# A decoder block on one core: attention rows turned four steps behind their scores, values ahead of the next pair's transposes

## The chip, the cores and the metric

The kernel runs on one core of a Trainium2 chip. A core has five engines, each with an instruction stream of its own: TensorE (PE in the profile, with PEld for its weight loads), VectorE (DVE), ScalarE (ACT), GpSimd (POOL), and SyncE (SP), which here issues the DMAs. They meet through semaphores. Matrix products go to PSUM, which this kernel cuts into eight banks of 128 x 512 float32; DVE and ACT read them from there. The metric is the device time of one launch in microseconds.

## The reference, cut to what matters

One decoder block on 512 tokens of width 1024: a norm, one projection, a retention branch and an attention branch, a gated merge, and a feed-forward part. The change lies in the attention branch alone, eight heads of 64:

```python
def forgetting_attention(q, k, v, log_f):
    scale = 1.0 / math.sqrt(d)
    c = jnp.cumsum(log_f, axis=1).transpose(0, 2, 1)
    ...
        s = jnp.einsum('bhqd,bhkd->bhqk', q_blk, kh).astype(jnp.float32) * scale
        s = s + c_blk[..., None] - c[:, :, None, :]
        mask = pos_k[None, :] <= pos_q[:, None]
        s = jnp.where(mask[None, None], s, -jnp.inf)
        p = jax.nn.softmax(s, axis=-1)
        return jnp.einsum('bhqk,bhkd->bhqd', p.astype(vh.dtype), vh)
```

## The kernel before

Float32 products are made of three products of a high and a low part each (`three`), so nearly every matmul runs as high x high, high x low and low x high.

The program is one stream on TensorE. From `pinned[0] = True` to `pinned[0] = False` the matmuls keep the order in which the code is written; where the code is not pinned, and on all other engines, a scheduler sets the order when the kernel is built, and each engine then works through its list in that order. The projection comes first, then retention, then attention (about 169 to 248 us of the profiled execution), then the merge and the feed-forward part.

Attention runs in steps `s`, one for each row block of one head: `chain` holds the 32 triples (a, e, i), pair `a` 0 to 3, head `e` 0 or 1 in the pair, block `i` of 128 queries from 3 down to 0. Here "row s" is the work on `chain[s]`, (i+1) x 128 columns wide. A row goes through these hands:

- `fox_scores` (L481): two matmuls into a bank tagged `sc` (there are two of these). DVE adds the bias row `cb` and takes the minimum (L499, a custom operation into `pr`, with `nm` read after it); ahead of it POOL adds the mask to one 128 x 128 square of `cb` (L491). ACT takes the exponential of `pr` in place (L501, with the row sums read after it), DVE takes the reciprocal `ri` (L502) and scales `pr` (L503).
- `fox_turn` (L506): TensorE transposes the i+1 squares of `pr` into a bank tagged `tp` (two of these as well, shared with `fox_prep`), and the bank is copied to `pT`: by DVE where i is 3 (L516), by ACT otherwise (L518).
- `fox_values` (L520): once both heads of a pair are turned, eight products of `pT` with `vf`, the two heads by turns, into an `sc` bank; ACT and DVE take it out (L171, L172, `ofh` and `ofl`). The first product of each head reads the part of `pT` that the last turned row, i = 0, writes.
- `fox_prep` (L458): for the next pair, at steps with `s % 8` of 3 and 5, TensorE transposes `kf` (part 0) or `qf` (part 1) into a `tp` bank. ACT copies halves of it out (`tk`, L467 and L468, four copies; `tq`, L477, two), and DVE makes the remainders (`kl`, L469; `tq`, L478, two each).

Between these, `fill(us)` puts other products into the stream: the projection's gate columns (`acc<-xh,wh` in the rows; `acc` names four further banks), whose inputs do not hang on attention. They last until step 20. The products of the next stage (`acc<-orh,...`, `acc<-ofh,...`) are not pinned, and the scheduler puts some of them into the stream from step 15 on. With the gate columns come weights, cast by ACT (`wh`, L152) and subtracted by DVE (`wl`, L153).

The loop at L629 says what a step does: scores of row s, at two steps in eight `fill` and `fox_prep`, the turn of row s - LAG with LAG = 3, the values of a pair at step 8a + 11, and a `fill`. `PT`, `PR` and `CBUF` are the numbers of buffers of `pT`, `pr` and `cb`.

Of the kernel before, what the change touches and what calls it, by code (L numbers as in the profile page):

```python
# [53 lines left out]
def block_kernel(ctx: ExitStack, tc, x, xT, c_early, c_tab, c_late, w_qf, w_tok, w_a, w_y, w_o, w_gu, w_dn, w_dh, out):  # L54
# [16 lines left out]
    def mm(o, **kw):  # L71
        in_order(nc.tensor.matmul(o, **kw))  # L72

    def turn(o, src):
        in_order(nc.tensor.transpose(out=o, in_=src, identity=ident))  # L75

    def f32(ap):
        return ap.bitcast(F32)
# [12 lines left out]
    def bank(tag):  # L91
        return ps.tile([P, 512], F32, name=tag, tag=tag, bufs={"acc": 4, "sc": 2, "tp": 2}[tag])
# [35 lines left out]


    WU, WP = 1056, 1152  # L130
    RAW, WB, SG, PT, PR, TB, CBUF = 2, 3, 8, 3, 4, 2, 3
    PREP = [3, 5]
    RF, CF, PF, SF, LAG = (5.32, 4.64, 5.6, 4.6, 11.2), (3.0, 2.0, 2.26, 4.0), 5.9, (0.83, 1.03, 1.77, 1.6), 3

    raw_pools, part_pools, turns = [wp] * RAW, [wp] * WB, [0, 0]

# [33 lines left out]
    def split_ps(src, h, l):  # L170
        nc.scalar.copy(out=h, in_=src)  # L171
        tt(out=l, in0=src, in1=f32(h), op=ALU.subtract)  # L172
# [282 lines left out]
    ra, rb = slice(0, FD), slice(FD, P)  # L455
    fox = {}

    def fox_prep(a, part):  # L458

        if part == 0:  # L460
            tk = [fwk.tile([P, S], F32R, name="tk", tag=f"tk{e}", bufs=TB) for e in range(2)]
            kl = kls[a % TB]
            pk = bank("tp")
            for t in range(NT):
                turn(pk[:, t * P:(t + 1) * P], kf[:, t, a * P:(a + 1) * P])
            for e, (r, o) in enumerate(((ra, rb), (rb, ra))):
                act(out=tk[e][r], in_=pk[r], func=AF.Copy, scale=gk[r])  # L467
                act(out=tk[e][o], in_=pk[r], func=AF.Copy, scale=gk[r])  # L468
                stt(out=kl[e][r], in0=pk[r], scalar=gk[r], in1=f32(tk[e])[r], op0=ALU.mult, op1=ALU.subtract)  # L469
            fox["k", a] = tk, kl  # L470
        else:
            tq = [fwk.tile([P, S], F32R, name="tq", tag=f"tq{e}", bufs=TB) for e in range(2)]
            pq = bank("tp")
            for t in range(NT):
                turn(pq[:, t * P:(t + 1) * P], qf[:, t, a * P:(a + 1) * P])
            for e, (r, o) in enumerate(((ra, rb), (rb, ra))):
                act(out=tq[e][r], in_=pq[r], func=AF.Copy, scale=gq[r])  # L477
                stt(out=tq[e][o], in0=pq[r], scalar=gq[r], in1=f32(tq[e])[r], op0=ALU.mult, op1=ALU.subtract)  # L478
            fox["q", a] = tq

    def fox_scores(a, e, i):  # L481

        tq, (tk, kl) = fox["q", a], fox["k", a]
        if i == NT - 1:
            fox["cb"] = fox_bias(2 * a + e)
            fox["pT", a, e] = fwk.tile([P, 3 * 384 + S], F32, name="pT", tag="pT", bufs=PT)
        cb = fox["cb"]
        n = (i + 1) * P
        m = max(n, 256)
        qs = slice(i * P, n)  # L490
        gp.tensor_tensor(out=cb[:, qs], in0=cb[:, qs], in1=mask, op=ALU.add)  # L491
        sc = bank("sc")
        mm(sc[:, :m], lhsT=tq[e][:, qs], rhs=tk[e][:, :m], start=True, stop=False)
        mm(sc[:, :m], lhsT=tq[e][:, qs], rhs=kl[e][:, :m], start=False, stop=True)
        pr = fwk.tile([P, S], F32, name="pr", tag="pr", bufs=PR)
        nm = sm.tile([P, 1], F32, name="nm", tag="nm", bufs=4)
        rs = sm.tile([P, 1], F32, name="rs", tag="rs", bufs=4)
        ri = sm.tile([P, 1], F32, name="ri", tag="ri", bufs=4)
        nc.vector.tensor_tensor_reduce(out=pr[:, :n], in0=cb[:, :n], in1=sc[:, :n], scale=-1.0, scalar=3e38,  # L499
                                       op0=ALU.add, op1=ALU.min, accum_out=nm)  # L500
        fox["last"] = act(out=pr[:, :n], in_=pr[:, :n], func=AF.Exp, scale=-1.0, bias=nm, accum_out=rs)  # L501
        nc.vector.reciprocal(out=ri, in_=rs)  # L502
        ts(out=pr[:, :n], in0=pr[:, :n], scalar1=ri, scalar2=None, op0=ALU.mult)  # L503
        fox["pr", a, e, i] = pr

    def fox_turn(a, e, i):  # L506

        pr, pT = fox["pr", a, e, i], fox["pT", a, e]
        pt = bank("tp")
        for j in range(i + 1):  # L510
            turn(pt[:, j * P:(j + 1) * P], pr[:, j * P:(j + 1) * P])
        row = pT[:, i * P:(i + 1) * P]
        dst = bass.AP(tensor=row.tensor, offset=row.offset, ap=[row.ap[0], [384, i + 1], [1, P]])
        src = pt[:, :(i + 1) * P].rearrange("p (j q) -> p j q", j=i + 1)
        if i == 3:
            nc.vector.tensor_copy(out=dst, in_=src)  # L516
        else:
            nc.scalar.copy(out=dst, in_=src)  # L518

    def fox_values(a):  # L520
        av = bank("sc")
        for j in range(NT):
            for e in range(2):
                mm(av[e * FD:(e + 1) * FD, j * P:], lhsT=vf[:, j, (2 * a + e) * FD:(2 * a + e + 1) * FD],
                   rhs=fox["pT", a, e][:, j * 512:j * 384 + 512], start=j == 0, stop=j == NT - 1)
        split_ps(av, ofh[:, a, :], ofl[:, a, :])
# [94 lines left out]
    for pair in kls:  # L621
        for e, o in enumerate((rb, ra)):
            gp.memset(f32(pair[e])[o], 0.0)
    fox_prep(0, 1)
    fill(CF[3])
    fox_prep(0, 0)
    fill(PF)
    chain = [(a, e, i) for a in range(4) for e in range(2) for i in reversed(range(NT))]
    for s in range(len(chain) + LAG + 2):  # L629
        if s < len(chain):  # L630
            fox_scores(*chain[s])
            if s % 8 in PREP and s // 8 < 3:
                fill(SF[0] / 2)
                fox_prep(s // 8 + 1, PREP.index(s % 8))
        if LAG <= s < len(chain) + LAG:
            fox_turn(*chain[s - LAG])
        v = s - LAG - 1
        if v >= 0 and v % 8 == 7:
            if v == 7:
                fill.until(2)  # L640
            fox_values(v // 8)
        fill(SF[chain[min(s, len(chain) - 1)][2]])
    fill.until(1)
    pinned[0] = False
# [284 lines left out]
    for g in range(4):  # L929
        if g < 3:  # L930
            ws.append(factors(w_dh[g + 1]))
        o = pf[:, HALF + 2 * g:HALF + 2 * g + 2, :].rearrange("p a (s t) -> p (a s) t", s=2)
# [135 lines left out]
```

## Time and profile before

| | |
|---|---|
| median of three timed runs | 716.09 us (715.72 to 716.59) |
| the profiled execution | 717.38 us, its span 715.6 us |
| TensorE busy | 708.9 us, 99% of the span |
| DVE, ACT, POOL busy | 509.2, 344.0, 70.1 us |
| granted TensorE clock | 1.000 over the span |

The span runs from the first to the last instruction; the rest of the time, 1.8 us, lies around it. The profiled execution was 1.3 us longer than the median. TensorE's busy time counts matmuls to their modelled ends, which overlap the next, so a short wait can hide in it; the distance from one matmul's start to the next one's shows it.

### The profile page before, as it was taken

What the parts mean: (1) busy time and instruction counts of PE and PEld (TensorE: products, weight loads), DVE (VectorE), ACT (ScalarE), POOL (GpSimd) and SP (SyncE); (2) the same over time, 40 slices, a digit from 0 to 9 for tenths busy, and PEclk for the clock granted to TensorE, in tenths of its full rate; (3) what the DMA queues carried; (4) which work ended last, traced back from release to release, by engine and by line L of the source; (5) the groups of instructions that cost most, each with busy time, mean ns of one, the idle gap of its engine ahead of it and who ended that gap; (6) DMA issues with size and microseconds to landing.
All of it is one profiled execution on the core that took longest, in us unless ns stands there. A gap on an engine that the chain in (4) does not pass through costs nothing.

```text
span 715.6 us, 10855 instructions
## 1 busy us (share of the span) xinstructions
PE 708.9 (99%) x4307; PEld 623.7 (87%) x4307; DVE 509.2 (71%) x844; ACT 344.0 (48%) x532; POOL 70.1 (10%) x90
## 2 busy tenths in 40 slices
PE   8999999999999999999999999999999999999998
PEld 6888998888777688888888999999999998888998
DVE  6333667756878673545968798899888998854684
ACT  4542434446766732233654755655665555533251
POOL 0163502121311100000220000000000000000000
PEclk9999999999999999999999999999999999999999
DMA  8632222233212023326603233322332213353112
GB/s 286 248 118 90 63 87 62 87 121 119 96 65 73 31 89 101 105 89 220 221 1 117 69 110 119 118 71 106 120 118 92 86 56 122 120 173 99 56 69 75
DMA packets 19908, 76.34 MB, mean 107 GB/s; under 512 B 2312, under 2 KB 2952, under 8 KB 16656
## 3 DMA queue, kind: packets, MB, share of 16 engines
q1 hardware_dynamic: 19712, 75.62, 31.2%
q8 instruction: 34, 0.56, 0.3%
q14 instruction: 18, 0.15, 0.1%
q10 hardware_dynamic: 144, 0.02, 0.0%
HBM read 73.52 MB, written 2.11 MB: 106 GB/s over the span
## 4 chain that ended last, share of the span: by engine, by line
PE 92%; DVE 3%; ACT 2%; issue 1%; POOL 1%; DMA 1%; SPq 0%; DVEq 0%; ACTq 0%
PE acc L72 59%; PE sc L72 27%; PE tp L72 5%; PE tp L75 2%; DVE pr L499 1%; POOL cb L491 1%; DVE pr L503 1%; DMA raw<-in_w_tok_dram 1%; ACT pr L501 1%; ACT tk L468 0%; DVE tq L478 0%; ACT tk L467 0%; DVE kl L469 0%; DVE sg L548 0%; DVE ofl L172 0%
## 5 line engine op out<-in xcount | busy, mean ns | idle before, releaser
L152 ACT CAST wh<-raw 128x1024 fp32r<-128x1024 f32 (+1 forms) x52 | 54.5, 1050 | 123.4 <-PE acc L72 97.4
L153 DVE TENSOR_TENSOR wl<-raw,wh 128x1024 fp32r<-128x1024 f32 (+1 forms) x52 | 66.6, 1282 | 48.4 <-ACT wh L152 48.3
L72 PE MATMUL sc<-xfh,cl 128*128 128x256 f32 x288 | 83.2, 289 | 0.0
L72 PE MATMUL sc<-xfh,ch 128*128 128x256 f32 x288 | 81.6, 283 | 0.0
L72 PE MATMUL sc<-xfl,ch 128*128 128x256 f32 x288 | 81.4, 283 | 0.0
L72 PE MATMUL acc<-wh,xh 128*128 128x512 f32 (+2 forms) x192 | 69.7, 363 | 0.0
L741 DVE TENSOR_TENSOR cl<-t,ch 128x1024 fp32r<-128x1024 f32 x48 | 58.6, 1222 | 13.7 <-ACT ch L741 13.6
L72 PE MATMUL acc<-wh,xl 128*128 128x512 f32 (+2 forms) x192 | 68.2, 355 | 0.0
L72 PE MATMUL acc<-wl,xh 128*128 128x512 f32 (+2 forms) x192 | 68.0, 354 | 0.0
L72 PE MATMUL acc<-xfh,ah 128*128 128x256 f32 (+1 forms) x216 | 63.9, 296 | 0.0
L72 PE MATMUL acc<-xfh,al 128*128 128x256 f32 (+1 forms) x216 | 63.7, 295 | 0.0
L72 PE MATMUL acc<-xfl,ah 128*128 128x256 f32 (+1 forms) x216 | 63.7, 295 | 0.0
L741 ACT CAST ch<-t 128x1024 fp32r<-128x1024 f32 x48 | 50.5, 1052 | 12.8 <-PE tp L72 8.0
L72 PEld LDWEIGHTS sc<-xfh,cl 128*128 128x128 f32 x288 | 55.0, 191 | 0.8 <-DVE cl L741 0.2
L72 PEld LDWEIGHTS sc<-xfh,ch 128*128 128x128 f32 x288 | 55.1, 191 | 0.1
L72 PEld LDWEIGHTS sc<-xfl,ch 128*128 128x128 f32 x288 | 55.1, 191 | 0.0
L72 PE MATMUL acc<-xh,wh 128*128 128x512 f32 x128 | 51.8, 404 | 0.0
L72 PE MATMUL acc<-xh,wl 128*128 128x512 f32 x128 | 50.0, 391 | 0.0
L72 PE MATMUL acc<-xl,wh 128*128 128x512 f32 x128 | 49.9, 390 | 0.0
L741 DVE TENSOR_TENSOR al<-raw,ah 128x1536 fp32r<-128x1536 f32 x24 | 42.2, 1757 | 6.9 <-ACT ah L741 6.9
L72 PEld LDWEIGHTS acc<-xfh,al 128*128 128x128 f32 x216 | 41.3, 191 | 1.0
L72 PEld LDWEIGHTS acc<-xfl,ah 128*128 128x128 f32 x216 | 41.3, 191 | 0.9
(294 smaller groups left out, 1796.3 us busy)
## 6 DMA issues: line engine op xcount, KB each, us to landing
raw<-in_w_gu_dram SPq DMA_DIRECT2D x21, 1024.0 KB, 4.8
raw<-in_w_tok_dram SPq DMA_DIRECT2D x16, 512.0 KB, 3.7
raw<-in_w_a_dram SPq DMA_DIRECT2D x16, 512.0 KB, 3.6
t<-in_w_dn_dram SPq DMA_DIRECT2D x14, 512.0 KB, 3.7
raw<-in_w_y_dram SPq DMA_DIRECT2D x8, 512.0 KB, 3.6
raw<-in_w_o_dram SPq DMA_DIRECT2D x8, 512.0 KB, 3.7
raw<-in_w_dh_dram SPq DMA_DIRECT2D x4, 1024.0 KB, 4.8
xf<-in_xT_dram SPq DMA_DIRECT2D x8, 256.0 KB, 5.0
```

The source lines that it names most:

```text
L72: in_order(nc.tensor.matmul(o, **kw))
L75: in_order(nc.tensor.transpose(out=o, in_=src, identity=ident))
L152: nc.scalar.copy(out=h[:, :width], in_=raw[:, :width])
L153: tt(out=l[:, :width], in0=raw[:, :width], in1=f32(h)[:, :width], op=ALU.subtract)
L491: gp.tensor_tensor(out=cb[:, qs], in0=cb[:, qs], in1=mask, op=ALU.add)
L499: nc.vector.tensor_tensor_reduce(out=pr[:, :n], in0=cb[:, :n], in1=sc[:, :n], scale=-1.0, scalar=3e38, op0=ALU.add, op1=ALU.min, accum_out=nm)
L501: fox["last"] = act(out=pr[:, :n], in_=pr[:, :n], func=AF.Exp, scale=-1.0, bias=nm, accum_out=rs)
L503: ts(out=pr[:, :n], in0=pr[:, :n], scalar1=ri, scalar2=None, op0=ALU.mult)
L741: split_to.last = nc.scalar.copy(out=h, in_=src), tt(out=l, in0=src, in1=f32(h), op=ALU.subtract)
```

## The change

Five edits. LAG goes from 3 to 4. In the loop, `fox_values` stands ahead of `fox_turn`; with the larger LAG the values of pair a come at step 8a + 12, behind the scores of that step and ahead of the turn of row 8a + 8. `pT` gets two buffers for three, `pr` six for four. In `fox_prep` the copies of a bank are all written ahead of the remainders.

```diff
-    RAW, WB, SG, PT, PR, TB, CBUF = 2, 3, 8, 3, 4, 2, 3
+    RAW, WB, SG, PT, PR, TB, CBUF = 2, 3, 8, 2, 6, 2, 3
     PREP = [3, 5]
-    RF, CF, PF, SF, LAG = (5.32, 4.64, 5.6, 4.6, 11.2), (3.0, 2.0, 2.26, 4.0), 5.9, (0.83, 1.03, 1.77, 1.6), 3
+    RF, CF, PF, SF, LAG = (5.32, 4.64, 5.6, 4.6, 11.2), (3.0, 2.0, 2.26, 4.0), 5.9, (0.83, 1.03, 1.77, 1.6), 4
@@ fox_prep
             for e, (r, o) in enumerate(((ra, rb), (rb, ra))):
                 act(out=tk[e][r], in_=pk[r], func=AF.Copy, scale=gk[r])
                 act(out=tk[e][o], in_=pk[r], func=AF.Copy, scale=gk[r])
+            for e, r in enumerate((ra, rb)):
                 stt(out=kl[e][r], in0=pk[r], scalar=gk[r], in1=f32(tk[e])[r], op0=ALU.mult, op1=ALU.subtract)
@@ 
             for e, (r, o) in enumerate(((ra, rb), (rb, ra))):
                 act(out=tq[e][r], in_=pq[r], func=AF.Copy, scale=gq[r])
+            for e, (r, o) in enumerate(((ra, rb), (rb, ra))):
                 stt(out=tq[e][o], in0=pq[r], scalar=gq[r], in1=f32(tq[e])[r], op0=ALU.mult, op1=ALU.subtract)
@@ the loop over s
-        if LAG <= s < len(chain) + LAG:
-            fox_turn(*chain[s - LAG])
         v = s - LAG - 1
         if v >= 0 and v % 8 == 7:
             if v == 7:
                 fill.until(2)
             fox_values(v // 8)
+        if LAG <= s < len(chain) + LAG:
+            fox_turn(*chain[s - LAG])
```

The number of instructions of each kind stays as it was; their order moves. TensorE's order from the scores of row 11 on, before (`acc` rows are gate columns, `sc<-tk` and `sc<-kl` scores, `tp<-ctab,kf` the transposes of k, `tp<-ctab,pr` turned rows, `sc<-pT` values):

```order
L72 MATMUL sc<-kl,tq 128x256
L75 MATMUL tp<-ctab,kf 128x128 x4
L75 MATMUL tp<-ctab,pr 128x128 x4
L72 MATMUL sc<-pT,vf 64x512 x2
L72 MATMUL sc<-pT,vf 64x384 x2
L72 MATMUL sc<-pT,vf 64x256 x2
L72 MATMUL sc<-pT,vf 64x128 x2
L72 MATMUL acc<-xh,wh 128x512
```

The same place in the changed kernel, up to the scores and the values:

```order
L75 MATMUL tp<-ctab,kf 128x128 x4
L75 MATMUL tp<-ctab,pr 128x128
L72 MATMUL acc<-xh,wh 128x512
L72 MATMUL acc<-xl,wh 128x512
L72 MATMUL acc<-xh,wl 128x512
L72 MATMUL acc<-xh,wh 128x512
L72 MATMUL acc<-xl,wh 128x512
L72 MATMUL acc<-xh,wl 128x512
L72 MATMUL sc<-tk,tq 128x512
L72 MATMUL sc<-kl,tq 128x512
L72 MATMUL sc<-pT,vf 64x512 x2
```

The values moved behind six gate matmuls and the scores of row 12; the last row of the pair, i = 0, is now turned right behind the transposes of k, and row 8 behind the values. At the same place of the next pair (step 20) three gate matmuls stand there for six, and three products of the next stage stand between the values' first and second product.

ACT's order there, before (`pr` the exponential, `tk` the copies of k, `pT` the copy of a turned row, `wh` a weight cast):

```order
L518 COPY pT<-tp 128x128
L501 ACTIVATE pr,rs<-pr,nm 128x256
L501 ACTIVATE pr,rs<-pr,nm 128x128
L467 ACTIVATE tk<-tp,ce 64x512
L468 ACTIVATE tk<-tp,ce 64x512
L467 ACTIVATE tk<-tp,ce 64x512
L468 ACTIVATE tk<-tp,ce 64x512
L171 CAST ofh<-sc 128x512
```

And in the changed kernel:

```order
L503 ACTIVATE pr,rs<-pr,nm 128x256
L503 ACTIVATE pr,rs<-pr,nm 128x128
L467 ACTIVATE tk<-tp,ce 64x512
L468 ACTIVATE tk<-tp,ce 64x512
L467 ACTIVATE tk<-tp,ce 64x512
L468 ACTIVATE tk<-tp,ce 64x512
L520 COPY pT<-tp 128x128
L503 ACTIVATE pr,rs<-pr,nm 128x512
L171 CAST ofh<-sc 128x512
```

The copy of the pair's last turned row (`pT`, 128x128) stood ahead of the exponentials of rows 10 and 11; it now stands behind them and behind the four copies of k. The same holds at step 19.

DVE's order around the transposes of q at step 13, before (`pr,nm` the custom operation, `sg` a gate column, `wl` a weight's low part):

```order
L503 TENSOR_SCALAR pr<-pr,ri 128x384
L478 SCALAR_TENSOR_TENSOR tq<-tp,gq,tq 64x512
L548 TENSOR_TENSOR sg<-acc,r_89 128x512
L153 TENSOR_TENSOR wl<-raw,wh 128x1024
L478 SCALAR_TENSOR_TENSOR tq<-tp,gq,tq 64x512
L499 ISA pr,nm<-cb,sc 128x256
```

And in the changed kernel:

```order
L505 TENSOR_SCALAR pr<-pr,ri 128x384
L550 TENSOR_TENSOR sg<-acc,r_89 128x512
L480 SCALAR_TENSOR_TENSOR tq<-tp,gq,tq 64x512 x2
L501 ISA pr,nm<-cb,sc 128x256
L501 ISA nm 128x1
L153 TENSOR_TENSOR wl<-raw,wh 128x1024
```

The two remainders of q stand together, and the custom operation of row 14 comes ahead of the weight's low part.

## Rows read from the trace of the kernel before

**Rows 1.** The page's first section: busy time of an engine, share of the span, instructions.

```profile
PE 708.9 (99%) x4307; PEld 623.7 (87%) x4307; DVE 509.2 (71%) x844; ACT 344.0 (48%) x532; POOL 70.1 (10%) x90
```

**Rows 2.** A window of ten microseconds late in attention: its stretch and length, PE, PEld, DVE, ACT and POOL busy (with instructions), granted clock, DMA share, GB/s.

```profile
223.00:233.00 10.00, 9.21 (x51) 6.73 (x50) 9.07 (x27) 7.26 (x20) 2.23 (x5) 1.00 0.16 52
```

**Rows 3.** The chain that ended last, in order of time: start, length, what. The piece that follows attention.

```profile
247.89 130.79 PE acc L72 x576
```

**Rows 4.** TensorE's timeline at the waits in attention: start, busy time to the modelled end, instruction, and in brackets the idle time before it with its releaser. Five pairs of an instruction and its next, then the values of the first and of the last pair.

```profile
177.78 0.39 PE L72 MATMUL sc<-kl,tq 128*128 128x512 f32 x1
178.21 0.55 PE L75 MATMUL tp<-ctab,pr 128*128 128x128 f32 x3
...
205.70 0.28 PE L72 MATMUL sc<-kl,tq 128*128 128x256 f32 x1
206.28 0.66 PE L75 MATMUL tp<-ctab,pr 128*128 128x128 f32 x4 [0.30 <-ACT pT L518]
...
207.47 0.40 PE L72 MATMUL acc<-orh,wh 128*128 128x512 f32 x1
208.11 0.51 PE L72 MATMUL sc<-tk,tq 128*128 128x512 f32 x1 [0.24 <-DVE nm L499]
...
225.02 0.40 PE L72 MATMUL acc<-orh,wh 128*128 128x512 f32 x1
226.01 0.33 PE L75 MATMUL tp<-ctab,pr 128*128 128x128 f32 x1 [0.59 <-ACT pT L518]
...
232.38 0.40 PE L72 MATMUL acc<-orh,wl 128*128 128x512 f32 x1
232.95 0.63 PE L75 MATMUL tp<-ctab,pr 128*128 128x128 f32 x4 [0.17 <-DVE pr L503]
...
241.34 0.40 PE L72 MATMUL acc<-ofh,wh 128*128 128x512 f32 x1
242.09 0.52 PE L75 MATMUL tp<-ctab,pr 128*128 128x128 f32 x3 [0.35 <-DVE pr L503]
...
194.76 2.37 PE L72 MATMUL sc<-pT,vf 128*64 128x512 f32 x16
...
244.82 3.07 PE L72 MATMUL sc<-pT,vf 128*64 128x512 f32 x16
```

**Rows 5.** TensorE's timeline around the first values: the transposes of k, a turned row of four squares, the first of six gate matmuls, the scores of row 12, the start of a turned row of three squares.

```profile
193.79 0.60 PE L75 MATMUL tp<-ctab,kf 128*128 128x128 f32 x4
194.23 0.60 PE L75 MATMUL tp<-ctab,pr 128*128 128x128 f32 x4
...
197.06 0.50 PE L72 MATMUL acc<-xh,wh 128*128 128x512 f32 x1
...
198.57 0.39 PE L72 MATMUL sc<-tk,tq 128*128 128x512 f32 x1
...
199.04 0.49 PE L75 MATMUL tp<-ctab,pr 128*128 128x128 f32 x3
```

**Rows 6.** ACT's timeline there: a copy of a turned row of one square (that of row 7), the exponential of row 11, the first and the last two of the four copies of k.

```profile
192.74 0.26 ACT L518 COPY pT<-tp 128x128 f32<-128x128 f32 x1
...
194.95 0.40 ACT L501 ACTIVATE pr<-pr,nm 128x128 f32<-128x128 f32 x1 [1.18 <-DVE nm L499]
...
195.35 0.67 ACT L467 ACTIVATE tk<-tp,ce 64x512 fp32r<-64x512 f32 x1
...
197.52 0.69 ACT L467 ACTIVATE tk<-tp,ce 64x512 fp32r<-64x512 f32 x1 [0.81 <-DVE kl L469]
198.22 0.68 ACT L468 ACTIVATE tk<-tp,ce 64x512 fp32r<-64x512 f32 x1
```

**Rows 7.** The same place of the third pair: TensorE's transposes of k, ACT's first copy of k.

```profile
215.67 0.60 PE L75 MATMUL tp<-ctab,kf 128*128 128x128 f32 x4
...
217.00 0.67 ACT L467 ACTIVATE tk<-tp,ce 64x512 fp32r<-64x512 f32 x1
```

**Rows 8.** DVE and POOL ahead of the exponential of row 11: a weight's low part, the custom operation of row 11; two of POOL's masks, the second that of row 11.

```profile
193.00 1.21 DVE L153 TENSOR_TENSOR wl<-raw,wh 128x1024 fp32r<-128x1024 f32 x1
...
194.56 0.29 DVE L499 CUSTOM_DVE_ANT_0 pr<-cb,sc 128x128 f32<-128x128 f32 x1 [0.27 <-POOL cb L491]
...
192.06 0.47 POOL L491 TENSOR_TENSOR cb<-cb,ctab 128x128 f32<-128x128 f32 x1 [0.48 <-DMA cb<-cd]
193.15 1.37 POOL L491 TENSOR_TENSOR cb<-cb,ctab 128x128 f32<-128x128 f32 x1 [0.63 <-DVE nm L499]
```

**Rows 9.** DVE at step 13 to 16: a weight's low part, the second remainder of q, the custom operation of row 14. Then the custom operation and the exponential of row 20.

```profile
205.59 1.22 DVE L153 TENSOR_TENSOR wl<-raw,wh 128x1024 fp32r<-128x1024 f32 x1
206.84 0.75 DVE L478 SCALAR_TENSOR_TENSOR tq<-tp,gq,tq 64x512 fp32r<-64x512 f32 x1
207.62 0.42 DVE L499 CUSTOM_DVE_ANT_0 pr<-cb,sc 128x256 f32<-128x256 f32 x1
...
221.99 0.68 DVE L499 CUSTOM_DVE_ANT_0 pr<-cb,sc 128x512 f32<-128x512 f32 x1
...
222.77 0.73 ACT L501 ACTIVATE pr<-pr,nm 128x512 f32<-128x512 f32 x1 [1.22 <-DVE nm L499]
```

## The prediction

> **What bounds the kernel now.** I read the page's first section, then windows by stage, then the chain that ended last, then the timelines of TensorE, ACT, DVE and POOL side by side. The first section shows TensorE busy for 99% of the span, the next engine, DVE, for 71% [rows 1]. The edits touch attention alone, and there the windows show the one stage with another near-limit: late in attention DVE is busy 9.07 us of ten while TensorE shows its gaps [rows 2]. The chain then tells what a gap costs: behind attention it is 576 TensorE products of the next stage in 130.79 us, 0.227 us each with no other engine between them [rows 3]. So what TensorE loses or gains in attention goes to the end of the span one for one, and nothing else does.
>
> The waits in attention are found on TensorE's timeline as the distance between two starts, less a step without a wait: 0.23 for 512 columns by the row above, 0.12 for 256 as half of it. They are [rows 4]: 0.20 at 177.78 (0.43 less 0.23), 0.46 at 205.70, 0.41 at 207.47, and in the tail 0.76 at 225.02, 0.34 at 232.38 and 0.52 at 241.34; the last values take 3.07 where the first take 2.37, 0.70 more. That is 3.4 us in all, which is the most that a better order of the same instructions can win.
>
> **The change part by part.** No instruction is added or dropped, so each cost is a wait made or a wait removed.
>
> *Values ahead of the turn, four steps behind (the loop, LAG).* The values' second product reads the part of `pT` that ACT writes from the pair's last turned row. Before, that copy was done at 193.00 (192.74 and 0.26) [rows 6], 1.8 us ahead of the first values at 194.76 [rows 4]. In the changed order it stands in ACT's list behind the exponential of row 11 and all four copies of k. So I walk both engines from the start of the transposes of k (193.79, [rows 5]).
> - ACT: the first copy of k starts at 195.35, 1.56 after that; four copies, of 0.67 to 0.69, take 2.74 without a wait between them; the copy of `pT` takes 0.26 [rows 6]. Ready at 1.56 + 2.74 + 0.26 = 4.56.
> - TensorE: transposes of k 0.44 (193.79 to 194.23), one square of row 7 at a quarter of that, 0.11, six gate matmuls 1.51 (197.06 to 198.57), scores of row 12 0.47 (198.57 to 199.04) [rows 5], the values' first product at 512 of the 2,560 columns of the first values, which take 2.30 to the next matmul (194.76 to 197.06, [rows 4, 5]), so 0.46. It arrives at 2.99.
> - The wait is 1.57.
>
> At the next pair the same walk goes from 215.67: the first copy of k starts 1.33 later [rows 7], ready at 4.33. TensorE has three gate matmuls for six (0.76) but three products of the next stage between the two products of the values (0.76): 0.44 + 0.11 + 0.76 + 0.47 + 0.46 + 0.76 = 3.00. The wait is 1.33. The third pair has no transposes of a next pair there, and the last has products of the next stage between its two; I put both at nothing. Sum **+2.9**.
>
> The bounds come from the one unknown, when the copies of k start. At the lowest they start when the transposes are done (0.60 after their start, the length of the row of four [rows 5]); then the waits are 0.61 and 0.60, 1.2 in all. That needs the exponential of row 11 about 1 us earlier. At the highest, ACT is as above and TensorE arrives 0.3 earlier at each place, an estimate: the one square (0.11) and half of the transposes' 0.44 may lie beside their neighbours; that makes 2.9 + 0.6 = 3.5. I take 2.9: the exponential of row 11 stands behind DVE's custom operation of that row, at 194.56, and this behind the weight's low part, 1.21 long from 193.00 [rows 8], and neither stands elsewhere in the changed order.
>
> Here a rule bears on the row. POOL's mask of row 11 takes 1.37 from 193.15, the one before it 0.47 [rows 8]; the long one lies beside that low part, a subtraction of two SBUF tensors. The Trainium skill, SBUF — State Buffer, "Who interferes with whom", says that such a DVE operation and a GpSimd read exclude each other over a shared port. The rows agree: 1.37 beside the low part, 0.47 without. By that rule the mask ends behind the low part in the changed kernel too. Without it the custom operation would still wait for the low part, to 194.21, and start 0.35 earlier, so that the two waits together would be some 2.5 for 2.9.
>
> *Larger LAG: a turn has one more step of time.* At 177.78 the wait goes, since no turn stands at the place any more: −0.20. In the tail each turn comes one step later against its scores, but DVE is nearly full there [rows 2], so part of the delay piles up all the same. What helps is at row 20: before, its custom operation ran at 221.99 and its exponential at 222.77 [rows 9]; now DVE's list has the custom operation ahead of the second remainder of k and of the values' remainder, and ACT reaches the exponential behind the copies of k and of `pT`, at 217.00 + 2.74 + 0.26 = 220.00, some 2.8 us earlier. The tail's waits are 0.76 + 0.34 + 0.52 + 0.70 = 2.3 [rows 4]. The first of them, 4 us behind row 20's exponential, I let go whole, and of the other 1.56, which lie 10 us and more later, a tenth, an estimate: **−0.9**. Bounds: 0 (DVE's sum unchanged, so the waits only move) and −2.3 (all gone).
>
> *Copies in one go.* The two remainders of q stand together at step 13, and row 14's custom operation comes ahead of a weight's low part. Before, low part 1.22, remainder 0.75 and custom operation stood in a line from 205.59 on [rows 9], and TensorE waited 0.46 and 0.41 at their ends [rows 4]. The custom operation, without that 1.22, is done early enough for both: **−0.87**; bounds 0 and −0.87. For k, the third copy waited 0.81 for the first remainder [rows 6]; now the four copies run through and the remainders follow. The bank is held from 195.35 to 199.70 before (the second remainder ends 0.80 behind the last copy), 4.35 us, and 2.74 + 2 x 0.75 = 4.24 now: nothing.
>
> *Two buffers of `pT`, six of `pr`.* The next pair's first turn stands behind the values on TensorE, so it can't ask for a third buffer any sooner; nothing. If its copies did wait, the next pair's turns would, some 0.3 us each. More of `pr` only frees DVE; nothing.
>
> Sum: 2.9 − 0.2 − 0.9 − 0.87 = +0.9. The profiled execution would go from 717.38 to 718.3; it was 1.3 longer than the median, so the median goes from 716.09 to **717.0**.
>
> **The rivals.**
> - *The copy of `pT` is in time* (faster). If ACT starts the copies of k as soon as they are turned, the values cost 1.2, and if the tail's waits also go, 1.2 − 0.2 − 0.87 − 2.0 = −1.9: 714.2. For it: in the one-go copies the 0.81 of waiting between the copies of k [rows 6] is gone, and I may have the start of the copies too late. Against it: the exponential of row 11 waited 1.18 for DVE [rows 6], not for TensorE. It decides from where the waits at the two values fall under 2.0 in sum. The Trainium skill, PSUM — Partial Sum Buffer, "Engine vs sequencer instructions", says that ScalarE's queue is strictly first in, first out. No row of before sets such a copy behind the copies of k, so none shows it for this pair. By that rule the copy can't pass them, and this rival has only the way by an earlier start. Chance 0.22.
> - *The waits come and nothing is given back* (slower). DVE's sum is the same in the tail, so its lateness is only shifted: 3.3 − 0.2 − 0.5 − 0.1 = +2.5, 718.6. For it: 9.07 of ten busy. Against it: row 20's exponential, 2.8 earlier. Chance 0.27.
> - *The waits swap* (my forecast), 715.7 to 718.0 by a few tenths on each term. Chance 0.46.
> - *Nothing of it is felt*, as the gate columns ahead take up the waits: the fill is cut in us, not in waits, so TensorE can't; 716.1. Chance 0.05.
>
> **How the numbers follow.** 0.2% of 716.09 is 1.43 us, about what a measurement of this kernel tells from no change: faster is under 714.66, slower over 717.52. The first rival gives 0.18 of its 0.22 to faster, the rest to same. The second is slower throughout. My forecast, 717.0 with 715.7 to 718.0 around it, lies under 717.52 with three parts in four: 0.34 same, 0.10 slower, 0.02 faster; and the last is same. That makes 0.20 faster, 0.43 same, 0.37 slower. The range runs from 714.3 (the first rival's middle, below which a tenth is left) to 719.1, past the second rival's middle.
>
> **What would show it.** Right: on TensorE's timeline, at steps 12 and 20, a gap of 1 to 2 us inside the values, behind their first product, released by ACT's copy of `pT`; no wait ahead of row 12's turn or row 16's scores; row 20's exponential about 2 us earlier against its scores; the tail's waits under 1.6. Wrong: values without a gap (then the copies of k started early, or ACT's queue was ahead), or a longer gap at the scores of steps 13 and 21, which would mean that the bank's release, and not the copy, is the price; or a tail with more waits than before, where DVE would be the bound.

## The result

The changed kernel takes 718.47 us (median of seven runs, 718.04 to 719.72), the kernel before 716.09 in the same session. The ratio is 1.0034, with a 95% interval of 1.0022 to 1.0045: 2.4 us slower. The forecast was 717.0 within 714.3 to 719.1. One profiled execution of the experiments (the copies by turns) took 1924.75 us where the other eleven of that kernel took 715 to 717, so its trace is left out.

The page's first section of the changed kernel, which answers to [rows 1], in the same columns:

```profile
PE 710.9 (99%) x4307; PEld 623.8 (87%) x4307; DVE 509.3 (71%) x844; ACT 344.9 (48%) x532; POOL 71.4 (10%) x90
```

The same 4307 matmuls, 2.0 us more of TensorE's time called busy. So the loss hides in "busy", and the sum of TensorE's waits does not show it. This is the view of waits of the changed kernel, TensorE from 170 to 250 us (what waited, for whom, us in total, times, the longest):

```profile
PE sc L72 <- ACT pT L520: 1.3, 2, 0.9
PE tp L75 <- ACT pT L520: 0.2, 1, 0.2
```

The two waits of the values are there, behind ACT's copy of `pT`, as forecast, but at 1.3 us together. TensorE's timeline shows what they cost. At step 12 of the changed kernel (answers to the values in [rows 4] and to [rows 5]; start, busy to the modelled end, instruction, idle time and its releaser):

```profile
193.22 0.60 PE L75 MATMUL tp<-ctab,kf 128*128 128x128 f32 x4
193.66 0.27 PE L75 MATMUL tp<-ctab,pr 128*128 128x128 f32 x1
...
195.15 0.40 PE L72 MATMUL sc<-tk,tq 128*128 128x512 f32 x1
195.39 0.39 PE L72 MATMUL sc<-kl,tq 128*128 128x512 f32 x1
195.71 1.07 PE L72 MATMUL sc<-pT,vf 128*64 128x512 f32 x2
197.64 2.37 PE L72 MATMUL sc<-pT,vf 128*64 128x512 f32 x14 [0.86 <-ACT pT L520]
199.94 0.66 PE L75 MATMUL tp<-ctab,pr 128*128 128x128 f32 x4
```

A product of the values is two records here, so `x16` in [rows 4] is the eight products. Before, they took 2.30 from the first start to the next matmul; now they take 4.23 (195.71 to 199.94). The trace marks only 0.86 idle. But the 14 records that are left behind the gap take 2.30 (197.64 to 199.94), as long as all 16 took before. The reason is in the starts of the single records: before, those of the two heads come in pairs, 0.006 us apart, the first at 194.758 and 194.764. The two heads write different halves of the bank's partitions and run side by side. The first head's early product saves nothing, since the second head still needs its own 2.30. So the rule for the values is: time = (second head's start less the first's) + 2.30. At step 12 this is 1.93 + 2.30.

Steps 20, 28 and 36 of the changed kernel, the same view:

```profile
217.77 1.07 PE L72 MATMUL sc<-pT,vf 128*64 128x512 f32 x2
218.77 0.50 PE L72 MATMUL acc<-orh,wh 128*128 128x512 f32 x1
...
220.17 2.37 PE L72 MATMUL sc<-pT,vf 128*64 128x512 f32 x14 [0.43 <-ACT pT L520]
222.47 0.66 PE L75 MATMUL tp<-ctab,pr 128*128 128x128 f32 x4
...
235.61 2.38 PE L72 MATMUL sc<-pT,vf 128*64 128x512 f32 x16
237.91 0.66 PE L75 MATMUL tp<-ctab,pr 128*128 128x128 f32 x4
...
245.03 1.07 PE L72 MATMUL sc<-pT,vf 128*64 128x512 f32 x2
...
247.16 2.37 PE L72 MATMUL sc<-pT,vf 128*64 128x512 f32 x14
249.45 0.50 PE L72 MATMUL acc<-ofh,wl 128*128 128x512 f32 x1
```

Step 20: 4.70, of which 2.30 is the pair's own and 0.69 three products of the next stage (3 x 0.23), so 1.71 lost. Step 28, where no transposes of a next pair stand, keeps its 2.30. The last values take 4.42 with four other products inside (0.92): 1.20 lost, where the kernel before lost 0.70, and the trace marks no idle time there at all.

ACT's timeline at step 12 (answers to [rows 6]):

```profile
194.14 0.40 ACT L503 ACTIVATE pr<-pr,nm 128x128 f32<-128x128 f32 x1 [1.22 <-DVE nm L501]
...
194.54 0.67 ACT L467 ACTIVATE tk<-tp,ce 64x512 fp32r<-64x512 f32 x1
195.22 0.68 ACT L468 ACTIVATE tk<-tp,ce 64x512 fp32r<-64x512 f32 x1
195.92 0.68 ACT L467 ACTIVATE tk<-tp,ce 64x512 fp32r<-64x512 f32 x1
196.61 0.68 ACT L468 ACTIVATE tk<-tp,ce 64x512 fp32r<-64x512 f32 x1
197.32 0.27 ACT L520 COPY pT<-tp 128x128 f32<-128x128 f32 x1
```

The row was turned at 193.66 and its copy runs at 197.32, 3.7 us later, behind four copies that nobody waits for so soon.

**Where the time went.** The table compares the starts of matmuls in the two traces at places where TensorE has issued the same set of matmuls in both (the differences are of unrounded times).

| up to | before | changed | difference | of that, new |
|---|---|---|---|---|
| ahead of attention | 110.69 | 110.21 | −0.47 | −0.47 |
| a turn at 184 | 184.12 | 183.56 | −0.56 | −0.09 |
| past the first values | 199.04 | 200.35 | +1.31 | +1.87 |
| step 15 | 206.28 | 207.39 | +1.10 | −0.21 |
| step 24 | 228.95 | 230.80 | +1.85 | +0.75 |
| end of attention | 247.82 | 249.79 | +1.97 | +0.12 |

The first line is nearly all from the first 11 us of the span, where nothing was changed. Attention itself lost 1.97 + 0.47 = 2.44 us, which is the 2.4 of the medians.

### The profile page after: what moved, and what is told of

It is laid out like the page before. It is cut to its first block, busy times and chain, and to the rows that moved or that the text cites. A ratio compares the mean times of both kernels' runs of the same rounds, so it can differ in the third digit from the quotient of the medians.

```text
span 717.5 us, 10846 instructions
## 1 busy us (share of the span) xinstructions
PE 710.9 (99%) x4307; PEld 623.8 (87%) x4307; DVE 509.3 (71%) x844; ACT 344.9 (48%) x532; POOL 71.4 (10%) x90
## 4 chain that ended last, share of the span: by engine, by line
PE 93%; DVE 2%; ACT 2%; issue 1%; POOL 1%; DMA 1%; SPq 0%; DVEq 0%; ACTq 0%
PE acc L72 59%; PE sc L72 27%; PE tp L72 5%; PE tp L75 2%; DVE pr L501 1%; POOL cb L493 1%; ACT pr L503 1%; ACT tk L468 1%; DMA raw<-in_w_tok_dram 1%; ACT tk L467 0%; DVE pr L505 0%; DVE sg L550 0%; DVE tq L480 0%; ACT wh L152 0%; DVE ri L504 0%
```

## The experiments

The times are ratios to the kernel before on the same chip, with 95% intervals. Two experiments are compared with each other by their ratios to it, and where their intervals overlap, the difference is one of the points alone.

**The transposes of k behind the turn.** The changed kernel, in the loop at L629:

```diff
-            if s % 8 in PREP and s // 8 < 3:
+            if s % 8 == PREP[1] and s // 8 < 3:
                 fill(SF[0] / 2)
-                fox_prep(s // 8 + 1, PREP.index(s % 8))
+                fox_prep(s // 8 + 1, 1)
 ...
         if LAG <= s < len(chain) + LAG:
             fox_turn(*chain[s - LAG])
+        if s % 8 == PREP[0] and s // 8 < 3:
+            fill(SF[0] / 2)
+            fox_prep(s // 8 + 1, 0)
```

> The changed kernel with one thing moved: at steps 3, 11 and 19 the transposes of the next pair's k stand behind the turn of that step, not ahead of it, so that ACT copies the pair's last turned row ahead of the four copies of k. First theory: the two heads' products of the values run side by side on TensorE, so whatever keeps the second head back is lost whole; 1.9 us at step 12 and 1.6 at step 20 (the second head's start less the first's, less the 0.8 of other products between) go away: 718.5 - 3.5 = 715.0, and both values take 2.3 us again. Rival: only the idle time that the trace marks ahead of the second head (0.86 and 0.43) goes, and the rest belongs to the values at their new place: 717.2.

Measured: 0.9986 (0.9977 to 0.9995), 1.0 us faster than the kernel before and 3.4 faster than the changed one. TensorE's and ACT's timelines at the first values:

```profile
195.56 2.37 PE L72 MATMUL sc<-pT,vf 128*64 128x512 f32 x16
197.87 0.66 PE L75 MATMUL tp<-ctab,pr 128*128 128x128 f32 x4
```
```profile
193.38 0.27 ACT L520 COPY pT<-tp 128x128 f32<-128x128 f32 x1 [0.59 <-PE tp L75]
...
194.42 0.67 ACT L467 ACTIVATE tk<-tp,ce 64x512 fp32r<-64x512 f32 x1
```

ACT's copy of that row ran at 193.38, ahead of the copies of k. The values are back at 2.31, at step 20 too. Of the 3.5 that I expected 3.4 came back, not only the idle time that the trace marked (1.3). The rival is out.

**The copy on another engine.** This tells ACT's list from the place of the transposes: TensorE's order is left alone.

```diff
-        if i == 3:
+        if i == 3 or (a < 2 and e == 1 and i == 0):
             nc.vector.tensor_copy(out=dst, in_=src)
```

> The changed kernel with the copy of the last turned row of the first two pairs (128x128) on DVE, not on ACT; TensorE's order stays as in the changed kernel, the transposes of k ahead of that turn. Theory: it is ACT's list that holds the second head back, and DVE is free there ahead of the custom operation of row 12, so both values take 2.3 again: 3.5 us faster than the changed kernel, 1.0 to 1.2 faster than the kernel before, as k_behind_turn. Rival: it is the place of the transposes of k ahead of the turn on TensorE, or DVE is as late as ACT, so that less than half of the 3.5 comes back: slower than the kernel before or level.

Measured: 0.9991 (0.9982 to 0.9999), 0.6 us faster than the kernel before, 3.1 faster than the changed one. DVE's and TensorE's timelines:

```profile
194.72 0.28 DVE L518 COPY pT<-tp 128x128 f32<-128x128 f32 x1
```
```profile
196.20 2.37 PE L72 MATMUL sc<-pT,vf 128*64 128x512 f32 x16
198.50 0.66 PE L75 MATMUL tp<-ctab,pr 128*128 128x128 f32 x4
```

Both values take 2.31. So it is ACT's list, not TensorE's order, that held the second head back.

**Half of the copies ahead.** The changed kernel with the two lines of the diff that part copies and remainders taken out again.

> The changed kernel with the copies by turns again (copy, copy, remainder): in ACT's list the copy of the pair's last turned row then stands behind two copies of k, not four. First theory: it is ready 2 x 0.69 = 1.4 us earlier, so the two values lose 0.5 and 0.2 for 1.9 and 1.6; the gain of the copies in one go (0.4 to 0.9) is lost: 718.5 - 2.8 + 0.6 = 716.3. Rival, the values lose by their place and not by the copy: 718.5 + 0.6 = 719.1.

Measured: 1.0013 (1.0004 to 1.0021), 0.9 us slower than the kernel before, 1.5 faster than the changed one. ACT's and TensorE's timelines at step 12:

```profile
194.03 0.68 ACT L468 ACTIVATE tk<-tp,ce 64x512 fp32r<-64x512 f32 x1
194.74 0.27 ACT L518 COPY pT<-tp 128x128 f32<-128x128 f32 x1
```
```profile
194.51 2.92 PE L72 MATMUL sc<-pT,vf 128*64 128x512 f32 x16
197.35 0.66 PE L75 MATMUL tp<-ctab,pr 128*128 128x128 f32 x4
```

The copy comes 1.4 earlier, and the values take 2.84: 0.54 lost for 1.93, as reckoned (0.5). At step 20 it is 1.0, where I had 0.2: with the copy due earlier, the scheduler no longer put the three other products between the heads. The time itself, 717.0 by the ratio, is between the two expectations and nearer the theory's 716.3. What the copies by turns cost with LAG 4 is also in this trace, on TensorE's timeline at steps 5 and 16:

```profile
178.35 0.60 PE L75 MATMUL tp<-ctab,qf 128*128 128x128 f32 x4
179.56 0.55 PE L75 MATMUL tp<-ctab,pr 128*128 128x128 f32 x3 [0.60 <-DVE kl L469]
...
205.23 0.40 PE L72 MATMUL acc<-xh,wl 128*128 128x512 f32 x1
206.13 0.50 PE L72 MATMUL sc<-tk,tq 128*128 128x512 f32 x1 [0.51 <-DVE nm L499]
```

The turn behind the transposes of q waits 0.77 for the remainders of k (1.21 less four squares of 0.11) where the changed kernel has 0.15, and the scores of step 16 wait 0.67 (0.90 less 0.23) where it has none: 1.3 us together.

**The heads in line.** The kernel before, in `fox_values`:

```diff
-        for j in range(NT):
-            for e in range(2):
+        for e in range(2):
+            for j in range(NT):
```

> The kernel before, with the values' eight products written head by head (four of the first, then four of the second) in place of by turns. If the two heads' products run side by side, each of the four values then takes about two times 2.3 us: 716.1 + 3 x 2.3 + about 1.6 at the last one, near 724.6. If they take turns on TensorE, nothing changes: 716.1.

Measured once: 721.12, 4.4 slower than the median of the kernel before in that session (716.71).

```profile
193.90 3.93 PE L72 MATMUL sc<-pT,vf 128*64 128x512 f32 x16
197.76 0.50 PE L72 MATMUL acc<-xh,wh 128*128 128x512 f32 x1
```

Each of the four values takes 3.86, not 2.30 and not the 4.6 that I expected. In the single records the second head starts 1.56 behind the first, before the first head is done, though all of its products stand behind the first head's in the list. 1.56 + 2.30 = 3.86: the rule holds, and I was wrong only on when the second head can start. The four values add 3 x 1.56 and 0.86 for the last, 5.5 in all, of which 4.4 is seen in the time: the waits that [rows 4] show at 205.70, 207.47 and 225.02 are smaller by 0.9 in this trace. So a loss in attention need not go to the end of the span whole, as the prediction had it: waits that lie behind it can take up a part.

**The copies in one go, alone.** The kernel before with the two lines of `fox_prep` from the diff.

> The kernel before with the copies written in one go and nothing else of the change. By the prediction the waits of 0.46 and 0.41 at steps 15 and 16 go: 716.1 - 0.9 = 715.2. Rival: the wait at step 15 stays (in the changed kernel it may have gone by the larger LAG alone), so 715.7; or a bank of k that comes free later gives it back: 716.1.

Measured: 1.0000 (0.9991 to 1.0009). The waits at steps 15 and 16 are gone, and the gain is given back, most of it at one place on TensorE's timeline:

```profile
204.23 0.28 PE L72 MATMUL sc<-kl,tq 128*128 128x256 f32 x1
205.06 0.33 PE L75 MATMUL tp<-ctab,pr 128*128 128x128 f32 x1 [0.55 <-ACT pT L520]
```

0.83 less the step of 0.12 is 0.71, a new wait. It needs a `tp` bank that ACT empties at 204.63 with a copy of `pT`, and that stands behind both copies of q (1.36 from 203.25). In the changed kernel, with a step more, the turns at that place do not wait for it.

**LAG back at 3.** The changed kernel with LAG at 3.

> The changed kernel with LAG back at 3, so that the values come at steps 11 and 19 again, right behind the transposes of k. Theory: the copy of the pair's last row stands ahead of the copies of k again, and both values take 2.3: 3.5 us faster than the changed kernel. But the copies in one go then make the wait of about 0.7 at step 14 that the run with them alone showed, and the first wait of the prediction (0.20) is back: 2.4 to 2.6 faster than the changed kernel, within 0.2 us of the kernel before. Rival: values ahead of the turn lose at any LAG: no faster than the changed kernel.

Measured: 1.0023 (1.0014 to 1.0032), 1.6 us slower than the kernel before, which neither expectation had. The values are at 2.30 again, so the theory holds that far, and the wait of 0.20 is back; the one of 0.7 at step 14 did not come. Others came instead. At 198.03 (and 219.00) a turn waits for the bank of k, which the copies in one go hold until both remainders are done:

```profile
197.08 0.39 PE L72 MATMUL sc<-kl,tq 128*128 128x512 f32 x1
198.03 0.52 PE L75 MATMUL tp<-ctab,pr 128*128 128x128 f32 x3 [0.55 <-DVE kl L470]
```

That is 0.95 less 0.23, 0.72, and 0.85 at step 20. And a last turn comes 1.0 late, as in the next run. In the trace attention is 0.9 longer than before; the timed runs say 1.6, and the 0.7 between them I can't place.

**Buffers.** k_behind_turn with `PT` 3 and `PR` 4.

> The kernel k_behind_turn with three buffers of the turned rows and four of the exponential, as before the change. The prediction put the buffers at nothing: same time as k_behind_turn to 0.3 us (1.0 faster than the kernel before). Rival: four buffers of the exponential hold DVE's custom operation back, now that a row lives a step longer: a wait of half a us or more at the scores of several steps, 1 to 3 us slower than k_behind_turn.

Measured: 0.9996 (0.9987 to 1.0005), 0.7 slower than k_behind_turn by the points, with intervals that overlap. No wait came at the scores. The trace shows another place, the last turn of the chain:

```profile
242.40 0.47 PE L72 MATMUL acc<-ofh,wl 128*128 128x512 f32 x1
243.90 0.33 PE L75 MATMUL tp<-ctab,pr 128*128 128x128 f32 x1 [1.03 <-ACT pT L520]
```

The bank that it needs is emptied by ACT behind a table load (1.28) for the next stage's sigmoids. In k_behind_turn the last two rows (three squares) are turned in one piece, without that wait. The late turn costs about 1.3 (1.50 from start to start, less 0.23); against that the last values lose 0.70 there and 1.20 in k_behind_turn. So in this trace "nothing" was right for what the buffers do to rows, and not for the order that the scheduler made at the end; that the time itself differs is not shown.

**The sigmoids behind the last copies.** `fox_turn` sets `fox["last"]`, behind which the sigmoids are ordered, in place of the exponential; on top of k_behind_turn, and alone on the kernel before.

```diff
-        fox["last"] = act(out=pr[:, :n], in_=pr[:, :n], func=AF.Exp, scale=-1.0, bias=nm, accum_out=rs)
+        act(out=pr[:, :n], in_=pr[:, :n], func=AF.Exp, scale=-1.0, bias=nm, accum_out=rs)
 ...
-            nc.scalar.copy(out=dst, in_=src)
+            fox["last"] = nc.scalar.copy(out=dst, in_=src)
```

> The changed kernel with the transposes of k behind the turn (as in k_behind_turn, 1.0 us faster than the kernel before by the medians' ratio) and one more thing: ACT takes the sigmoids of the merge, with their table load of 1.28, behind the copies of the last turned rows, not between them. Theory: the last values lose by the start of their second head, 2.1 us behind the first in the trace of k_behind_turn with 1.1 of other products between, so 0.9 to 1.0 comes back: 1.9 us faster than the kernel before, 714.2 against 716.1. Rival: the last turn, and not the copy, is late (DVE scales the last two rows only at 240.7 to 241.2), so at most 0.3 comes back; or the merge waits for its sigmoids and pays it again.

> The kernel before with the sigmoids behind the copies of the last turned rows and nothing else. Theory: its last values took 3.00 to the next matmul for 2.30, the second head starting 0.70 behind the first; with the copies first that goes: 0.7 us faster than the kernel before. Rival: it is the last turn that is late, so nothing; or the turn at 242.09, which waited 0.52 and stands on DVE, takes it up.

Measured: 0.9977 (0.9969 to 0.9986) for the first, 1.65 us faster than the kernel before and some 4 faster than the changed one: the best here by the points. Alone it gives 0.9997 (0.9988 to 1.0005), nothing that can be told. TensorE and ACT at the end of attention in the first:

```profile
240.05 0.52 PE L75 MATMUL tp<-ctab,pr 128*128 128x128 f32 x3
240.50 2.96 PE L72 MATMUL sc<-pT,vf 128*64 128x512 f32 x16
243.39 0.50 PE L72 MATMUL acc<-ofl,wh 128*128 128x512 f32 x1
```
```profile
240.50 0.54 ACT L520 COPY pT<-tp 128x256 f32<-128x256 f32 x2 [0.69 <-PE tp L75]
241.06 1.28 ACT L668 ACT_TABLE_LOAD   x1
```

The values take 2.89: the second head starts 0.59 late, which is about the length of ACT's two copies (0.54), and no other work of ACT lies between them. It lost 1.20 without the edit, so 0.6 came back of the 0.9 to 1.0 that I expected. In the kernel before it was 0.70, so only 0.1 was to be had, and I had put the whole 0.70 on ACT.

**The copies by turns, and LAG at 5,** both on the best kernel.

> The kernel k_turn_sig (1.65 us faster than the kernel before) with the copies of k and q by turns with their remainders again. The prediction put 0.9 us on the copies in one go at steps 15 and 16, and the traces of the changed kernel show 0.7 of it: so 0.7 to 0.9 slower than k_turn_sig. Rival: with LAG at 4 the waits at steps 15 and 16 are gone without it, and the copies in one go hold the bank of k or ACT longer: level or faster.

> The kernel k_turn_sig with LAG at 5 for 4. If the tail's waits come from too little time between a row's scores and its turn, the waits left in steps 20 to 35 (0.47, 0.32 and 0.23 in the trace of k_turn_sig) go: about 1 us faster than k_turn_sig. If they come from the sum of DVE's work, they stay or only move, and the last turns come a step later with nothing behind their scores to fill the time: level to 1 us slower.

Measured: 0.9992 (0.9983 to 1.0001) by turns and 0.9988 (0.9980 to 0.9997) with LAG 5, by the points 1.1 and 0.8 us slower than the best kernel, with intervals that overlap. That the copies in one go are worth about 1.1 with LAG 4 agrees with the 1.3 of waits that the trace of half of the copies ahead shows, on the changed kernel. With LAG 5 the waits left in the tail fall (0.47, 0.32 and 0.23 to 0.23 and 0.18, with a new one of 0.30 at the scores of 232.00: 1.0 to 0.7). But the turn behind the transposes of q at step 5 waits 0.7 (at 180.79), for 0.16 in the best kernel, and later the transposes of q wait 1.2 (1.40 less 0.17) for the bank of a turned row:

```profile
218.23 0.34 PE L72 MATMUL sc<-kl,tq 128*128 128x384 f32 x1
219.63 0.55 PE L75 MATMUL tp<-ctab,qf 128*128 128x128 f32 x3 [1.06 <-ACT pT L520]
```

So a small part of the tail's waits was time between scores and turn, and not DVE's sum alone; the two banks of `tp` then take the gain.

## Why the prediction was right and where it was wrong

Right was the mechanism and the direction: the copy of the pair's last row behind the copies of k makes TensorE wait at steps 12 and 20, what the other edits win is less, and all of it goes to the end of the span. The size was off: +0.9 forecast, +2.4 measured. 718.47 lies inside the range, because that reaches past the second rival's middle, but above the 715.7 to 718.0 that I gave the likeliest one, and the chances had slower at 0.37, not first. It stands at the second rival's 718.6, though not by the second rival's way alone. By terms:

| term | forecast | measured in the traces |
|---|---|---|
| values, steps 12 and 20 | +2.9 | +1.93 + 1.71 = +3.64 |
| wait of 0.20 at 177.78 | −0.20 | −0.09 |
| copies in one go (steps 15 and 16) | −0.87 | −0.21 − 0.41 = −0.62 |
| larger LAG, the tail | −0.9 | −0.43 |

The tail is what is left of the +0.87 from step 15 on: 0.87 − 1.71 + 0.41. The terms make 2.50 where the two traces differ by 2.44; the 0.06 lies in small differences of steps around the first values.

**The values: "it arrives at 2.99".** ACT's side was nearly right. The first copy of k started 1.32 behind the transposes (193.22 to 194.54) where I had 1.56, and the copy of `pT` was ready at 197.59, 4.37 for 4.56. The step that failed is TensorE's: I let it arrive behind the values' first product and took that 0.46 off the wait. It is not off the wait, since the heads run side by side. Without it the walk gives 1.57 + 0.46 = 2.03 and 1.33 + 0.46 = 1.79, near the 1.93 and 1.71. The Trainium skill, TensorE: Matmul & The Clock Gate, "The mechanism", says that matmuls at different tile positions of the array run at the same time; the pairs 0.006 us apart agree. The sign for it was in [rows 4]: the values are `128*64` where the other products are `128*128`. The bounds of 1.2 to 3.5 moved ACT's start and let TensorE arrive 0.3 earlier at most; they missed this, and 3.64 lies above them.

**The strict queue.** The copy of `pT`, turned at 193.66, ran at 197.32 behind four others, which agrees with the rule of the Trainium skill, PSUM — Partial Sum Buffer, "Engine vs sequencer instructions", that I cited against the first rival. That rival had no part in it: the copies of k started earlier than I reckoned by 0.24, not by 1. What the prediction took for the start of those copies held too: POOL's mask of row 11 was long again, 1.53 from 192.19 to 193.72, beside a weight's low part that ended at 193.41, and DVE's custom operation followed at 193.75.

**The tail: "I let go whole".** The wait of 0.76 at 225.02 is gone, as forecast: row 20's exponential runs at 220.15 (220.00 reckoned). The tail gave 0.43 back and not 0.9. The last values lost 1.20 for 0.70, and without that the tail would have given 0.93. I read their 0.70 as a wait that more time would shorten; it was the second head's start again, behind a table load of ACT (in the changed kernel 1.28 from 244.34), and with the larger LAG it grew. The runs with the sigmoids behind the copies show the place. That the rest comes to 0.9 is luck: the waits of 0.34 and 0.52, of which I let go a tenth, are gone too, and new ones stand for them, 0.34 at the turn of 228.57, 0.27 at the scores of 234.48 and 0.20 at the last turn. The larger LAG was not run by itself, so its share of this is not shown.

**The copies in one go.** 0.62 of 0.87 came; half of the rest is a longer step at the turn of 207.30 (0.25 for 0.12). What I had not seen is that this edit pays only with the larger LAG: alone it is worth nothing, and at LAG 3 with the values ahead a turn waits for the bank of k. The bank of k at 4.24 us for 4.35 was right on the length (4.30, from 194.54 to 198.84) and left out who asks for the bank next. That with LAG 4 it also shortens a wait at step 5, which the copies by turns make there, I had not seen either.

**The second rival's condition.** It ("nothing is given back") was wrong in its mechanism: 0.62 + 0.43 + 0.09 = 1.1 was given back.

## What to carry to other kernels

Before taking time off a wait because some work runs ahead of it, ask whether that work shares TensorE with what waits, or would have run beside it: here a product that ran early saved nothing, and the trace called most of the loss busy. Look for the cost in the distance between a group's first start and the start of what follows it, and not in the idle column. When values move behind or ahead of a turn, look at the in-order list of the engine that copies the turned row: transposes of k that moved four copies ahead of one copy, at two places, cost 3.6 us, and writing them behind the turn won 1.0 over the kernel before, 1.65 together with the sigmoids.

## What the runs showed of the hardware that I had not expected

Two chains of 64-column products to different halves of a bank run side by side for their whole length: 2.30 us for eight products as for four. In the heads-in-line run a product of the second head started 1.56 us behind the first head's start, ahead of the first head's last products (its second 256-column record started 1.77 and its last 128-column one 2.10 behind), although all of these stand ahead of it in the order in which the code is written. So "works through its list in that order", as it is said of every engine above, does not hold for the starts of such products.
